# Roped queries and key of latent attention: another row order in DRAM scratch, and weight requests moved into the rope stage

## The chip, the cores and the metric

The kernel runs on one core of a Trainium2 chip. Its time is the device time of one execution in microseconds (us); lower is better. Engines are named as in the profile: PE is the tensor engine (PEld its weight loads), DVE the vector engine, ACT the scalar engine, POOL the GpSimd engine, SP the sync engine. SP computes nothing here and issues transfers; ACT and POOL issue some too, between their own instructions. The engines run side by side, each takes its own instructions in a fixed order, and an instruction that waits holds up all that stand behind it on its engine.

## The reference

Two transformer blocks in float32, one sequence of 512 tokens, width 1024. The change touches only the first layer's mixer, multi-head latent attention with 16 heads:

```python
def mla_mixer(x, positions, cos, sin, w_in, q_norm, kv_norm, w_uq, w_uk, w_uv, w_o):
    h = x @ w_in
    c_q, c_kv, k_r = jnp.split(h, [MLA_Q_LORA, MLA_Q_LORA + MLA_KV_LORA], axis=-1)
    c_q = rms_norm(c_q, q_norm)
    c_kv = rms_norm(c_kv, kv_norm)
    q = (c_q @ w_uq).reshape(B, S, MLA_HEADS, MLA_NOPE + MLA_ROPE)
    q_nope = q[..., :MLA_NOPE]
    q_rope = apply_rope(q[..., MLA_NOPE:], cos[:, :, None], sin[:, :, None])
    k_rope = apply_rope(k_r, cos, sin)
    k_nope = (c_kv @ w_uk).reshape(B, S, MLA_HEADS, MLA_NOPE)
    v = (c_kv @ w_uv).reshape(B, S, MLA_HEADS, MLA_V)
    ...
        s = (jnp.einsum('bqhd,bkhd->bhqk', q_nope[:, q0:q1], k_nope[:, :q1])
             + jnp.einsum('bqhr,bkr->bhqk', q_rope[:, q0:q1], k_rope[:, :q1])).astype(jnp.float32) * scale
    ...
    return (o @ w_o).astype(x.dtype)
```

Each head's score is a sum over 128 plain dimensions and 64 roped ones. The roped key is one for all heads. Behind this mixer follow layer norms, a convolutional feed-forward layer, a second layer with gated linear attention, and a second block with attention, a recurrence and 16 experts; the change leaves all of that alone.

## The kernel before

Every float32 operand of a product is split into a leading part (hi) and an exact rest (lo). A product is three passes on PE, hi\*hi + hi\*lo + lo\*hi (`mm3`, lines 287 to 293). Weights come from DRAM into one of three raw buffers of 128 x 2048 (`load`, line 280, queue SP), and ACT (line 94) and DVE (line 95) split them piece by piece into one of five pairs `wh`, `wl`. A raw buffer is given back when its last piece is split, a pair when its last product is done. `next(w)` forces the split of what a product needs; `prime(n)` asks for the next n tiles early, if a buffer and a pair are free.

Attention (`mla`) runs in this order. The first product (`w_mla_in`) gives the query latents (4 tiles), the key and value latents (2 tiles) and the roped part of the key, each normed and split. The key's part is roped on 64 partitions (lines 537 to 539), copied to the other 64 (line 540) and split, so that `ks`, hi and lo, holds it twice over the partitions. Then the rope stage, `mla_rope`, runs for four groups of four heads. Its two products of 12 matmuls give x1 and x2 of four heads, 32 dimensions each, so that a tile's partition is head\*32 + dimension. DVE rotates them (lines 605 to 610), ACT and DVE split them (lines 270 and 271), and four transfers on SP (line 613) write hi x1, hi x2, lo x1, lo x2 to the scratch `q_dram`, where a head owns 128 rows: 32 of each part, one part behind the other. The head stage follows, 16 times: `mla_qk` reads the head's 128 rows from `q_dram` (line 622, SP) and makes query and key from `w_qk`; `mla_scores` multiplies (lines 666 to 670; the last two use the rows from `q_dram` and `ks`), takes the row maximum (line 676), the exponential (line 679) and the quotient (line 681) for four query tiles of 128, 256, 384 and 512 keys; `mla_transpose` turns the result (line 694) and splits it; `mla_values` multiplies with the values. The next head's query and key are made between a head's scores and its transposes.

`w_qk` is loaded two heads at a time (768 KB), `w_uv` four heads at a time, both through the same raw buffers as the rope weights. On each queue the order of the instructions is set when the program is built, by a scheduler that goes by when it expects buffers and engines to be free; what is asked for earlier in the code tends to be issued earlier. A transfer's wait can also be for an earlier transfer with which it shares a completion semaphore: there are eight of these for the transfers of SP and ACT together, taken in turn. The eight transfers of the input `xT` at the start of the head stage (line 550) are issued on ACT's queue.

Names in the rows below: `ps` a PSUM bank, `r` and `b` slots of 128 x 512 for split operands or float data, `f` quarters of float buffers, `wh`, `wl` weight parts, `raw` raw weights.

Of the kernel before, what the change touches and what calls it, by code (L numbers as in the profile page):

```python
# [55 lines left out]
# columns of the per-channel parameters, 128 channels to a column  # L56
# [10 lines left out]
class Weights:  # L67
    """Weights [group][128, units] taken tile by tile, `kt` units to a tile; split into parts in pieces of some units,
    a piece given back when its last tile is done."""
# [32 lines left out]
    # split what the next n tiles need, as far as there is room  # L102
# [11 lines left out]
class WeightTile:  # L114
# [9 lines left out]
    # all of its units, of a tile in one piece  # L124
# [6 lines left out]
    # of its units up to k  # L131
# [8 lines left out]
class Feed:  # L140
    """Tiles of several weights in a given order, the next ones being split while one is used."""
# [14 lines left out]
class Kern:  # L156
# [66 lines left out]
    # pairs of neighbouring slots: held, they aren't given out one by one; taken, they are out of the pool  # L223
# [40 lines left out]
    # hi keeps the leading mantissa bits that one float32r pass carries, lo is the exact rest  # L264
# [21 lines left out]
    # passes hi*hi + hi*lo + lo*hi  # L286
# [8 lines left out]
    # one output tile (of the depth tiles ks), for the tokens t0..t1  # L295
# [9 lines left out]
    # feature-major product, weights stationary. The first `lead` tiles leave the last depth tiles, which  # L305
    # come late, for the end; the first `head` and last `tail` tiles go by token halves.
    # then: the weights that come next
# [37 lines left out]
    # (v + eps)^-1/2: exp(-ln/2) with one Newton step  # L345
# [8 lines left out]
    # one function table for logarithms and exponentials  # L354
# [3 lines left out]
    # v^-1/2 of a small tile: the exponent halved in integers, then Newton steps  # L358
# [12 lines left out]
    # sum over the partitions of the squares of the tiles, times the value held in `ones`;  # L371
    # the tensor engine takes the squares by groups, of which VectorE makes the sums
# [18 lines left out]
    # layer norm of r without its bias, in r; h, l: the split of the whole  # L391
# [27 lines left out]
    # rms norm of x (kept); h, l the split of the result  # L419
# [15 lines left out]
    # ------------------------------------------------------------------  # L435
    def setup(self):
# [16 lines left out]
        # alpha * ln1 bias  # L453
# [3 lines left out]
    # cos and sin of positions * inv_freq, feature-major; also the block mask  # L457
    def rope_tables(self):
# [19 lines left out]
        # chunk ids; bias[q, k] = -1e30 where the key's chunk lies beyond the query's  # L478
# [13 lines left out]
    def mla(self, q_dram, after):  # L492
# [41 lines left out]
        # roped key, twice over the partitions, hi and lo  # L534
# [5 lines left out]
        nc.scalar.activation(kr[64:], k1, AF.Copy)  # L540
        ks = self.split_new(kr)
        self.free(kr, kt)
# [41 lines left out]
    # output projection of four heads, added to the residual; a tile at a time  # L584
# [13 lines left out]
    # roped parts of four heads' queries, scaled and split, to DRAM as [hi x1; hi x2; lo x1; lo x2] of each head  # L598
    def mla_rope(self, g, st):
        nc, w = self.nc, st["wr"]  # L600
        dst = st["q_dram"].rearrange("(g h i p) n -> g i h p n", g=4, h=4, i=4)
        cos, sin = st["cs"]
        pa = [self.mtile(next(w), 4, st["cq"]) for _ in range(2)]
        ra, rb, t1, t2 = self.Fs(4)
# [29 lines left out]
    # values of two heads, token-major, two token tiles to a slot  # L634
# [13 lines left out]
    # softmax of the scores; key tiles up to the query's  # L648
# [65 lines left out]
    def ffn(self, layer, ups, r, xh, xl, after):  # L714
# [4 lines left out]
        # m: 2 * i for the value, 2 * i + 1 for the gate  # L719
# [38 lines left out]
        for part, kt in enumerate(FF_PARTS):  # L758
# [4 lines left out]
            # one value and gate ahead of the product that waits for the last hidden tile  # L763
# [14 lines left out]
    # x + sigmoid(x @ w_gate + b) * (p @ w_proj); r, without the bias b2, is overwritten  # L778
# [38 lines left out]
    def gla(self, w, xh, xl, r_dram, after):  # L817
# [10 lines left out]
        # decays: log-sigmoids cumulated within each chunk  # L828
# [26 lines left out]
        def ev(m, ps, t0, t1):  # L855
            p, j = divmod(m, 4)
            h = 2 * p + j % 2
            if j < 2:
                q[h] = self.F()
                nc.scalar.activation(q[h], ps, AF.Copy, scale=float(128 ** -0.5))  # L860
            else:
                # decayed keys, token-major
                nc.vector.tensor_tensor(kd[h], kd[h], ps, ALU.mult)
                ps = self.ps("at")
                for t in range(4):
                    nc.tensor.transpose(ps[:, t * P:t * P + P], kd[h][:, t * P:t * P + P], self.ident)
                kdt[h] = self.F()
                nc.vector.tensor_copy(kdt[h], ps)
                self.free(kd[h])
# [4 lines left out]
        def turned(p, t, oc):  # L874
            # [chunk, half of the values, head, token]
# [9 lines left out]
        # states of two heads over the chunks; outputs normed, feature-major  # L885
        def recurrence(p, v):
# [18 lines left out]
            for n in range(8):  # L905
# [4 lines left out]
                # a head to each half of the partitions, a chunk to each half of the columns  # L910
# [63 lines left out]
        # the decays' first product, 16 columns wide: next to their hi parts the lo parts, which so need no pass  # L974
# [34 lines left out]
    def first_block(self, q_dram, r_dram, done):  # L1009
# [3 lines left out]
        for layer in range(2):  # L1013
# [13 lines left out]
            if layer == 0:  # L1027
                r = self.mla(q_dram, ln1)
            else:
                r = self.gla(w_gla, *x, r_dram, ln1)  # L1030
# [22 lines left out]
    # ------------------------------------------------------------------  # L1053
    # token-major copy of x, to DRAM
# [12 lines left out]
    # lambda on every partition  # L1067
# [18 lines left out]
    # rope tables with the norm gains in them: A = [g1 c | g2 c], B = [g1 s | -g2 s] for q and k  # L1086
# [32 lines left out]
    # token-major product of 256 columns, two token tiles to a bank  # L1119
# [11 lines left out]
    # queries and keys of a head: roped with their gains; keys are normed, queries are left to the scores' scale  # L1131
    def qk_head(self, w, then, h, tabs, st):
# [9 lines left out]
        for tp in range(2):  # L1142
            # [token, (tile of the pair, q or k, sub-head, dim)]
# [12 lines left out]
            # hi and lo parts; the transposes stack queries as [hi; hi] and [lo; lo], keys as [hi; lo]  # L1156
# [89 lines left out]
    # rms norm of each head's output over its value dimension  # L1246
# [16 lines left out]
    # softplus(-lambda) * 8, with log1p as an odd series in e / (2 + e)  # L1263
    def lru_consts(self):
# [19 lines left out]
        # half of 8 * softplus, and its negative; half biases  # L1284
# [7 lines left out]
    # gated recurrences of one tile of 128 channels; sigmoids as (1 + tanh) / 2  # L1292
    def lru_tile(self, m, px, pg, raw, y_dram):
        nc, a = self.nc, self.a
        sp, nsp, ba, bi = self.lru_c
        # 2 * gelu(g) = g * (1 + tanh(sqrt(2/pi) (g + 0.044715 g^3)))
# [17 lines left out]
        for d in range(2):  # L1314
# [9 lines left out]
            # z = 8 softplus r; a = exp(-z), 1 - a^2 = tanh(z) (1 + a^2)  # L1324
# [22 lines left out]
    # the recurrent branch, and of the gates as many tiles as FILL_GATES  # L1347
# [21 lines left out]
    # 2 * sigmoid - 1 of one tile of the gates  # L1369
# [12 lines left out]
    def second_block(self, x, h, o_dram, y_dram, g_dram):  # L1382
# [45 lines left out]
        # 2 * sigmoid as 1 + tanh; the halves are taken when merged is split  # L1428
# [32 lines left out]
    # the first block and its norm, x to DRAM token-major, then the second block up to the merged branches  # L1461
    def blocks(self, q_dram, r_dram, xtok, o_dram, y_dram, g_dram):
# [7 lines left out]
        x = self.first_block(q_dram, r_dram, done)  # L1470
        return self.second_block(x, h, o_dram, y_dram, g_dram)

    # ------------------------------------------------------------------
    # x + merged @ w_out, token-major, then its rms norm and the routing
    def out_and_route(self, mh, ml, w, xtok, out):
# [22 lines left out]
        # sum with x, its squares, its part of the router's products without the norm  # L1498
# [62 lines left out]
    def route_setup(self):  # L1561
# [12 lines left out]
        # the last slot less the token id, and its negative  # L1574
# [11 lines left out]
    # one-hot of the first position that holds the maximum  # L1586
# [9 lines left out]
    # group and experts of the tokens of a tile, their places in the experts' queues  # L1596
    def route(self, t, lg, rs):
# [14 lines left out]
        # the two experts of every group, the group of every token  # L1612
# [7 lines left out]
        # an expert's tokens from the first slot on, the others from the last one down  # L1620
# [9 lines left out]
    # weights of the two experts: softmax over them, times the group's probability  # L1630
    def route_weights(self):
# [19 lines left out]
        # token id, one, weight hi, weight lo  # L1651
# [5 lines left out]
    # tokens of the fullest expert  # L1657
# [9 lines left out]
    # [token, slot] of four experts, 1 where the token sits in the slot  # L1667
# [14 lines left out]
    # tokens of the slots, feature-major, split; token ids and weights of the slots  # L1682
    def dispatch(self, g, oh):
        nc = self.nc
        x = []
        for k in range(8):
            # of the first group, some tiles already have the tokens that are routed first
# [17 lines left out]
    # product of an expert's tokens with one of its two first matrices  # L1705
# [36 lines left out]
    # the first products of an expert run before the last of the expert before  # L1742
# [33 lines left out]
    # experts with more tokens than the slots of the first pass: the further slots, 128 at a time  # L1776
# [207 lines left out]
```

## Time and profile before

| what | value |
|---|---|
| median of 3 runs | 2432.88 us (2431.99 to 2433.94) |
| span of the profiled execution | 2430.5 us |
| PE busy | 2359.0 us (97%) |
| DVE busy, ACT busy, POOL busy | 1675.9, 1300.3, 50.1 us |
| mean granted clock of PE | 0.989 of full speed |
| HBM read, written | 286.00 MB, 25.17 MB |

For the profiled execution the page gives the span from its first to its last instruction and no other time; the span is 2.4 us below the median of the runs. PE is busy nearly throughout: in the page's 40 slices of 61 us it has nines everywhere but in the first two and the last, and the second slice, with 5, is the lowest. A busy share of PE near 1 says that the order of the work behind it passes on any shift in time unchanged.

### The profile page before, as it was taken

To read this page: it belongs to the slowest core of one execution; us is meant where nothing else is said; L and a number is where in the kernel's file an instruction comes from. 1 tells how busy PE (TensorE), PEld (TensorE's weight loads), DVE (VectorE), ACT (ScalarE), POOL (GpSimd) and SP (SyncE) were. 2 spreads that over 40 slices of the span, in tenths; PEclk is the share of its full clock that TensorE was granted. 3 is DMA by queue.
4 is the path that set the end of the run, shared out by engine and by line. 5 is a ranking of instruction groups with operands and counts; after the bars stand their busy time and mean duration, and the time that the engine had idled before them with its cause. 6 is when DMAs were issued, how large, how long until landed. Compare 5 with 4: busy or idle time off the path is not lost. (4 is left out here: it accounts for less than half of the span.)

```text
span 2430.5 us, 31858 instructions
## 1 busy us (share of the span) xinstructions
PE 2359.0 (97%) x12252; PEld 1987.2 (82%) x12252; DVE 1675.9 (69%) x3236; ACT 1300.3 (54%) x2048; POOL 50.1 (2%) x52
## 2 busy tenths in 40 slices
PE   8599999999999999999999999999999999999997
PEld 6488888888889776798888899888888778788886
DVE  7476668646466645585554578888888664989876
ACT  5154444434245523353332466777777843678776
POOL 0000000000000000000000000000000000011001
PEclk9799999999999999999999999999999999999999
DMA  5421221232222322312222213222323254489887
GB/s 182 146 76 66 78 100 41 99 109 100 104 96 88 118 78 83 117 70 98 104 93 104 98 69 123 101 91 76 118 70 109 74 199 165 176 310 380 300 302 246
DMA packets 62475, 313.26 MB, mean 129 GB/s; under 512 B 7504, under 2 KB 8144, under 8 KB 33904
## 3 DMA queue, kind: packets, MB, share of 16 engines
q1 hardware_dynamic: 49200, 279.73, 31.6%
q0 software_dynamic: 4864, 16.78, 2.7%
q10 hardware_dynamic: 8256, 14.68, 2.0%
q8 instruction: 98, 1.61, 0.3%
q14 instruction: 57, 0.47, 0.1%
HBM read 286.00 MB, written 25.17 MB: 128 GB/s over the span
## 5 line engine op out<-in xcount | busy, mean ns | idle before, releaser
L291 PE MATMUL ps<-r,wh 128*128 128x512 f32 (+1 forms) x2352 | 865.2, 371 | 14.0 <-ACT r L268 7.6
L293 PE MATMUL ps<-r,wl 128*128 128x512 f32 (+1 forms) x2352 | 862.3, 368 | 2.7 <-DVE wl L95 2.6
L292 PE MATMUL ps<-r,wh 128*128 128x512 f32 (+1 forms) x2320 | 851.9, 368 | 1.1 <-DVE r L269 0.5
L94 ACT ACTIVATE wh<-raw 128x1024 fp32r<-128x1024 f32 (+2 forms) x416 | 426.9, 1033 | 564.5 <-PE ps L292 433.4
L95 DVE TENSOR_TENSOR wl<-raw,wh 128x1024 fp32r<-128x1024 f32 (+2 forms) x416 | 491.6, 1191 | 213.5 <-ACT wh L94 206.5
L291 PEld LDWEIGHTS ps<-r,wh 128*128 128x128 f32 x2352 | 444.1, 190 | 92.6 <-ACT r L268 8.0
L293 PEld LDWEIGHTS ps<-r,wl 128*128 128x128 f32 x2352 | 444.5, 189 | 75.8 <-DVE wl L95 4.2
L292 PEld LDWEIGHTS ps<-r,wh 128*128 128x128 f32 x2320 | 438.9, 190 | 75.2 <-issue 3.9
L291 PE MATMUL ps<-wh,r 128*128 128x512 f32 (+1 forms) x944 | 325.6, 345 | 0.0
L292 PE MATMUL ps<-wl,r 128*128 128x512 f32 (+1 forms) x944 | 323.1, 342 | 1.9 <-DVE wl L95 1.9
L293 PE MATMUL ps<-wh,r 128*128 128x512 f32 (+1 forms) x944 | 323.6, 343 | 0.0
L292 PEld LDWEIGHTS ps<-wl,r 128*128 128x128 f32 x944 | 179.3, 190 | 23.0 <-DVE wl L95 2.6
L291 PEld LDWEIGHTS ps<-wh,r 128*128 128x128 f32 x944 | 179.2, 190 | 21.1 <-issue 1.2
L293 PEld LDWEIGHTS ps<-wh,r 128*128 128x128 f32 x944 | 179.2, 190 | 20.6 <-issue 0.8
L95 DVE TENSOR_TENSOR wl<-f,wh 128x1024 fp32r<-128x1024 f32 x96 | 113.7, 1222 | 10.2 <-ACT wh L94 8.9
L94 ACT ACTIVATE wh<-f 128x1024 fp32r<-128x1024 f32 x96 | 98.8, 1059 | 19.9 <-PE ps L293 19.9
L268 ACT ACTIVATE r<-ps 128x512 fp32r<-128x512 f32 (+1 forms) x141 | 76.0, 572 | 59.5 <-PE ps L293 42.1
L269 DVE TENSOR_TENSOR r<-ps,r 128x512 fp32r<-128x512 f32 (+1 forms) x132 | 83.4, 657 | 32.6 <-ACT r L268 32.4
L268 ACT ACTIVATE r<-f 128x512 fp32r<-128x512 f32 (+1 forms) x105 | 60.9, 589 | 59.5 <-DVE f L744 23.5
L269 DVE TENSOR_TENSOR r<-f,r 128x512 fp32r<-128x512 f32 (+1 forms) x105 | 65.7, 637 | 30.6 <-ACT r L268 28.1
L743 ACT ACTIVATE f<-f 128x512 f32<-128x512 f32 x39 | 24.7, 633 | 73.0 <-DVE f L727 72.9
L724 ACT ACTIVATE f<-ps,par 128x512 f32<-128x512 f32 (+1 forms) x78 | 56.8, 731 | 9.3 <-PE ps L293 9.3
(530 smaller groups left out, 2795.2 us busy)
## 6 DMA issues: line engine op xcount, KB each, us to landing
raw<-w_ffn_up SPq DMA_DIRECT2D x44, 1024.0 KB
f<-w_exp_in SPq DMA_DIRECT2D x33, 1024.0 KB
raw<-w_exp_in SPq DMA_DIRECT2D x31, 1024.0 KB
raw<-w_exp_dn SPq DMA_DIRECT2D x17, 1024.0 KB
raw<-w_ffn_dn SPq DMA_DIRECT2D x16, 1024.0 KB
f<-w_exp_dn SPq DMA_DIRECT2D x15, 1024.0 KB
raw<-w_gla SPq DMA_DIRECT2D x17, 512.0 KB
raw<-w_mla_o SPq DMA_DIRECT2D x8, 1024.0 KB
```

Source lines behind the costliest of these rows:

```text
L94: k.nc.scalar.activation(h, src, AF.Copy)
L95: k.nc.vector.tensor_tensor(l, src, h.bitcast(F32), ALU.subtract)
L268: nc.scalar.activation(h, src, AF.Copy)
L269: return nc.vector.tensor_tensor(l, src, h.bitcast(F32), ALU.subtract).ins
L291: self.nc.tensor.matmul(out, ah, bh, start=f, stop=False)
L292: self.nc.tensor.matmul(out, ah, bl, start=False, stop=False)
L293: self.nc.tensor.matmul(out, al, bh, start=False, stop=e)
L724: nc.scalar.activation(t[:, t0:t1], ps, AF.Identity, bias=self.col("conv_b", layer * m2 + ch), scale=w(2))
L743: nc.scalar.activation(g, g, AF.Gelu_apprx_tanh)
```

## The change

It has three parts.

1. The order of rows in the scratch: a head's 128 rows are now ordered by dimension first and part last (dimension\*4 + part). Each of the four writes of a group then covers 128 rows at a step of four, one run from partition 0 to 127, where it was four blocks of 32 rows.
2. The roped key has to have its rows in the same order. It is split on 64 partitions into `kp`, written from POOL's queue to a new scratch `k_dram` in eight transfers of 32 rows (each part once for the query's hi and once for its lo), and read back in two transfers of 128 rows into `ks`. The copy to the other 64 partitions is gone.
3. Within `mla_rope`, the third and fourth group ask for the first and the first two tiles of `w_qk` once their products are issued.

Lines that only held comments are emptied, so the code behind shifts by up to nine lines.

```diff
-        nc.scalar.activation(kr[64:], k1, AF.Copy)
-        ks = self.split_new(kr)
-        self.free(kr, kt)
+        kp, ks = self.Rs(2), self.Rs(2)
+        self.split(k1, kp[0][:64], kp[1][:64])
+        kd = k_dram.rearrange("(z p j i) n -> z j i p n", z=2, j=2, i=2)
+        for z in range(2):
+            for j in range(2):
+                for i in range(2):
+                    nc.gpsimd.dma_start(kd[z, j, i], kp[z][i * 32:i * 32 + 32].bitcast(F32))
+            nc.gpsimd.dma_start(ks[z].bitcast(F32), k_dram[z * P:z * P + P, :])
+        self.free(kr, kt, kp)
...
     def mla_rope(self, g, st):
         nc, w = self.nc, st["wr"]
-        dst = st["q_dram"].rearrange("(g h i p) n -> g i h p n", g=4, h=4, i=4)
+        dst = st["q_dram"].rearrange("(g p i) n -> g i p n", g=4, i=4)
         cos, sin = st["cs"]
         pa = [self.mtile(next(w), 4, st["cq"]) for _ in range(2)]
+        if g > 1:
+            st["wqk"].prime(g - 1)
```

How the rows move on SP, from the end of the rope stage of the kernel before (L613 are the writes of roped queries, L622 the read of one head's rows, L280 a load of weights):

```order
L622 DMA r_85<-q_dram 128x512
L613 DMA q_dram<-r_87 4x32x512
L613 DMA q_dram<-r_91 4x32x512
L613 DMA q_dram<-r_89 4x32x512
L613 DMA q_dram<-r_93 4x32x512
L280 DMA raw_69<-w_qk 128x1536
L280 DMA raw_67<-w_uv 128x1024
L280 DMA raw_68<-w_mla_o 128x2048
```

The same place now (the write is L622, the read L631):

```order
L622 DMA q_dram<-r_87 128x512
L280 DMA raw_69<-w_qk 128x1536
L622 DMA q_dram<-r_85 128x512
L622 DMA q_dram<-r_89 128x512
L280 DMA raw_68<-w_qk 128x1536
L631 DMA r_89<-q_dram 128x512
L622 DMA q_dram<-r_91 128x512
L280 DMA raw_67<-w_uv 128x1024
L622 DMA q_dram<-r_95 128x512
```

The load of `w_qk` for heads 4 and 5 stood behind all 16 writes (`raw_69`) and stands now behind 12 of them (`raw_68`); the one for heads 2 and 3, which was issued ahead of the rope stage, is now `raw_69`, behind ten.

On ACT, where the rope stage begins, before (L268 splits the key, L270 the roped queries, L94 weights; L550 are transfers of `xT`):

```order
L94 ACTIVATE wh_74<-raw_67 128x512
L540 ACTIVATE b_123<-b_123 64x512
L550 DMA f_80<-xT 128x512
L268 ACTIVATE r_113<-b_123 128x512
L270 ACTIVATE r_115<-f_82 128x512
```

and now (the transfers of `xT` are L556):

```order
L94 ACTIVATE wh_74<-raw_68 128x768
L268 ACTIVATE r_113<-b_123 64x512
L556 DMA f_80<-xT 128x512
L556 DMA b_123<-xT 128x512
L94 ACTIVATE wh_76<-raw_67 128x512
L270 ACTIVATE r_117<-f_82 128x512
```

The split of the first values' weights, `wh_76`, now stands ahead of the first split of roped queries; its pair is in use until the second group's products are done. Further on, at the first head's softmax, ACT before (L268 splits key and values, L679 is the exponential):

```order
L268 ACTIVATE r_94<-ps_129 128x512
L679 ACTIVATE f_84,s_680<-f_84,s_679 128x128
L679 ACTIVATE f_84,s_680<-f_84,s_679 128x384
L679 ACTIVATE b_122,s_680<-b_122,s_679 128x256
L94 ACTIVATE wh_74<-raw_69 128x768
L679 ACTIVATE f_84,s_680<-f_84,s_679 128x512
```

and now (the exponential is L688):

```order
L268 ACTIVATE r_98<-ps_129 128x512
L94 ACTIVATE wh_76<-raw_68 128x768
L688 ACTIVATE f_84,s_692<-f_84,s_691 128x128
L688 ACTIVATE f_84,s_692<-f_84,s_691 128x384
L688 ACTIVATE b_122,s_692<-b_122,s_691 128x256
L688 ACTIVATE f_84,s_692<-f_84,s_691 128x512
```

The split of the weights of head 4 (`wh_74<-raw_69` before, `wh_76<-raw_68` now) moved from ahead of the fourth exponential to ahead of the first. From the middle of the head stage to the end of the program the order on all engines is the same, but for buffer numbers.

## Rows read from the trace of the kernel before

**Rows 1.** Waits of the computing engines, 50 to 140 us: total us, times, longest.

```profile
PE ps L694 <- DVE f L681: 30.0, 1, 30.0
...
ACT wh L94 <- DMA raw<-w_qk: 30.0, 1, 30.0
...
ACT wh L94 <- DMA q_dram<-r: 8.1, 1, 8.1
...
DVE b L271 <- ACT b L270: 4.9, 1, 4.9
...
PE ps L291 <- DVE b L608: 2.4, 1, 2.4
```

**Rows 2.** Timeline of ACT, 60 to 123 us: start, duration, instruction, idle time before it.

```profile
60.59 0.64 ACT L268 ACTIVATE r<-b 128x512 fp32r<-128x512 f32 x1
62.33 0.64 ACT L270 ACTIVATE r<-f 128x512 fp32r<-128x512 f32 x1 [1.10 <-DVE f L609]
...
122.21 0.84 ACT L94 ACTIVATE wh<-raw 128x768 fp32r<-128x768 f32 x1 [30.01 <-DMA raw<-w_qk]
122.96 0.71 ACT L679 ACTIVATE f<-f,s 128x512 f32<-128x512 f32 x1
```

**Rows 3.** Timeline of SP's queue, 62 to 110 us.

```profile
62.99 4.70 SPq L613 DMA_DIRECT2D q_dram<-r  x4
...
105.99 3.06 SPq L613 DMA_DIRECT2D q_dram<-r  x4
109.15 2.74 SPq L280 DMA_DIRECT2D raw<-w_qk  x1
```

**Rows 4.** Windows: length; busy us (instructions) of PE, PEld, DVE, ACT, POOL; clock; DMA share; GB/s.

```profile
95.26:125.26 30.00, 0.00 (x0) 0.00 (x1) 1.47 (x4) 3.03 (x6) 0.00 (x0) 0.56 0.43 155
125.26:129.40 4.14, 4.14 (x13) 3.46 (x14) 3.36 (x6) 1.36 (x3) 0.00 (x0) 0.50 0.01 2
129.40:133.50 4.10, 4.10 (x29) 3.96 (x28) 1.69 (x7) 0.66 (x2) 0.00 (x0) 1.00 0.00 0
80.90:85.00 4.10, 3.66 (x12) 2.75 (x13) 4.07 (x7) 2.29 (x4) 0.00 (x0) 0.59 0.45 105
140.00:200.00 60.00, 60.00 (x336) 52.53 (x335) 43.41 (x122) 30.14 (x66) 0.00 (x0) 1.00 0.25 83
72.00:74.00 2.00, 2.00 (x10) 1.69 (x9) 2.00 (x4) 0.00 (x0) 0.00 (x0) 1.00 0.26 101
806.00:808.00 2.00, 2.00 (x11) 1.65 (x10) 2.00 (x4) 0.47 (x2) 0.00 (x0) 1.00 1.00 350
```

**Rows 5.** Timeline of SP's queue, 804 to 807 us: a weight load and a write of 128x512.

```profile
804.14 0.33 SPq L280 DMA_DIRECT2D raw<-w_gla  x1
806.68 0.32 SPq L1045 DMA_DIRECT2D r_dram<-f  x1
```

**Rows 6.** Timeline of PE, 90 to 126 us: scores, next head's query and key, transposes.

```profile
90.22 0.40 PE L670 MATMUL ps<-r,r 128*128 128x512 f32 x1
90.45 0.39 PE L291 MATMUL ps<-r,wh 128*128 128x512 f32 x1
...
94.54 0.27 PE L694 MATMUL ps<-ident,f 128*128 128x128 f32 x1
...
94.97 0.27 PE L694 MATMUL ps<-ident,f 128*128 128x128 f32 x1
125.26 1.33 PE L694 MATMUL ps<-ident,f 128*128 128x128 f32 x5 [30.02 <-DVE f L681]
```

**Rows 7.** Timeline of DVE: the maximum of the first head's fourth tile.

```profile
91.47 0.68 DVE L676 CUSTOM_DVE_ANT_0 f<-ps,f 128x512 f32<-128x512 f32 x1
```

**Rows 8.** Timeline of POOL: its first transfer, and a later one.

```profile
1476.30 0.75 POOL L1064 DMA_DIRECT2D xtok<-f  x1 [1475.84 <-ACT f L1063]
...
1536.56 0.54 POOL L1364 DMA_DIRECT2D g_dram<-f  x1 [38.38 <-ACT f L1375]
```

**Rows 9.** Landing of POOL's eight writes of 256 KB to one scratch.

```profile
DMA to landing us min/median/max: 2.3/2.3/5.5
```

More of the change, by code (lines that the diff above doesn't have):

```diff
@@ L489, in rope_tables, with mla @@
         return cos, sin, bias, fs
-    def mla(self, q_dram, after):
+    def mla(self, q_dram, k_dram, after):
         nc, a = self.nc, self.a
@@ L1007, in gla, with first_block @@
         return r
-    def first_block(self, q_dram, r_dram, done):
+    def first_block(self, q_dram, k_dram, r_dram, done):
         a = self.a
@@ L1027, in first_block @@
             if layer == 0:
-                r = self.mla(q_dram, ln1)
+                r = self.mla(q_dram, k_dram, ln1)
             else:
@@ L1459, in second_block, with blocks @@
         return mh, ml, w_out
-    def blocks(self, q_dram, r_dram, xtok, o_dram, y_dram, g_dram):
+    def blocks(self, q_dram, k_dram, r_dram, xtok, o_dram, y_dram, g_dram):
         h = []
@@ L1469, in done @@
             self.store_tokens(r, xtok, t0, t1)
-        x = self.first_block(q_dram, r_dram, done)
+        x = self.first_block(q_dram, k_dram, r_dram, done)
         return self.second_block(x, h, o_dram, y_dram, g_dram)
@@ L1850, in body @@
         new = lambda n, rows, cols: dram.tile([rows, cols], F32, tag=n, name=n)
-        q_dram, xtok = new("q_dram", 16 * P, S), new("xtok", S, D)
+        q_dram, k_dram, xtok = new("q_dram", 16 * P, S), new("k_dram", 2 * P, S), new("xtok", S, D)
         r_dram, o_dram, y_dram = (new(n, D, S) for n in ("r_dram", "o_dram", "y_dram"))
         g_dram = new("g_dram", 2 * D, S)
-        m = k.blocks(q_dram, r_dram, xtok, o_dram, y_dram, g_dram)
+        m = k.blocks(q_dram, k_dram, r_dram, xtok, o_dram, y_dram, g_dram)
         k.rings(mm=4, lg=1, at=3)
```

## The prediction

> **What bounds the kernel now.** I read the slices of the page first: PE is at nine tenths or more nearly everywhere, with one hole in the second slice. Then windows around it: PE runs no instruction in 30.00 us, and then 4.14 us at a granted clock of 0.50 (the level of 1.2 GHz) before it is back at 1.00 (2.4 GHz) [rows 4]. Further on, from 140 us, PE is full in every microsecond of the head stage [rows 4]. So the hole's length is the question.
>
> The list of waits then says who holds whom [rows 1]. PE's transposes wait 30.0 us for DVE's quotient (L681). That waits for the fourth exponential, and this one stands on ACT behind a weight split that waits 30.0 us for a load of `w_qk`. The timelines date it: the split starts at 122.21 and the exponential right behind it [rows 2], the last five transposes at 125.26 [rows 6]. The load was issued on SP at 109.15, behind the last four writes of roped queries (from 105.99) [rows 3]. So the bound is SP's queue.
>
> Why the writes are slow stands in the windows: with nothing but writes of the form 4x32x512 under way (72 to 74 us) the transfer engines are 0.26 busy and move 101 GB/s; at 806 to 808 us, with a weight load and a write of 128x512 issued shortly before [rows 5], they are 1.00 busy and move 350 GB/s [rows 4]. There are sixteen writes of 128 x 512 values of four bytes, four to a group. At 101 GB/s one takes 262144 / 101000 = 2.6 us, all sixteen 41.5 us. They begin at 62.99, and 62.99 + 41.5 = 104.5 is about where the last group is issued [rows 3].
>
> **The change part by part.** *The writes.* Each covers 128 rows now. By the row of 806 us, 256 KB at 350 GB/s take 0.75 us, sixteen 12 us. The step of four rows in DRAM is in no row; the bounds are 101 and 350 GB/s, and I take 350, since in the old form too the runs in DRAM are 2 KB rows, and what differs between the two windows is the share of the engines (a quarter, or all). Here the Trainium skill bears ("DMA: Bandwidth & Descriptors", section "Why a DMA increments its semaphore by 16 and not by 1"): a transfer is spread over the largest number of engines, up to 16, that divides the slowest dimension of both sides. By that rule the old form gets 4 of 16 and the new one 16; the share of 0.26 agrees for the old one, and by it the sixteen would take about a quarter of 41.5 us, 10 us.
>
> *The load that ends the wait.* On SP it stands behind 12 writes, not 16. What it must wait for is the split of the piece that was in its buffer, and the writes ahead of it, each of which waits for its own split on ACT and DVE. In the old trace ACT and DVE were themselves held back by slow writes: ACT waited 8.1 us for one at a shared semaphore, DVE 4.9 us for ACT, and PE 2.4 us for DVE [rows 1]. PE had worked without a gap up to 80.9 - 2.4 = 78.5 [rows 1, 4], at 0.227 us a matmul (18 of them from 90.45 to 94.54 [rows 6]); so the products of the third group, with 36 matmuls behind them (24 of the fourth, 12 of the first query), end at 70.3. Some ten instructions of DVE at 0.68 us [rows 7] split that group and the weights in its buffer, by about 77.5. The load is then out before 80, and 768 KB at 350 GB/s take 2.2 us. It lands before 86, and ACT needs it at about 87, ahead of the first exponential (the scores' last matmul is followed by the next product at 90.45 [rows 6]). So this wait goes.
>
> *What is late next.* For the last five transposes it is either PE's own work or the softmax of the fourth tile. In the old run PE had finished everything ahead of them at 94.97 + 0.27 = about 95.3 [rows 6], with the wait of 2.4 us in it. The softmax: DVE's maximum of the fourth tile ends at 91.47 + 0.68 = 92.15 [rows 7], and from the exponential's start to the transposes it took 125.26 - 122.96 = 2.3 us [rows 2, 6]; with one weight split of 0.84 us [rows 2] in between, 95.3. Both say 95.3, so 125.26 - 95.3 = **30.0 us** go. Without the wait of 2.4 us PE would be there at 92.9.
>
> *The clock.* After the hole PE ran 4.14 us at 0.50. Without a hole this is done in half: **2.1 us** go. Before it, too, PE was slow: 0.59 from 80.90 to 85.00, behind the wait of 2.4 us [rows 4]; at full clock that costs 4.10 x 0.41 = 1.7 us less. I leave it in, for the following reason.
>
> *The order on ACT and PE.* The split `wh_76` now stands ahead of the first split of roped queries, which ran at 62.33 [rows 2]. Its pair is free when the second group's products end. That is 24 matmuls of 0.227 us before 70.3, at 64.9, so the split of the first group's queries moves to about 65.7, 3.3 us later. DVE takes its work in order and is nearly full here, so its reading of the banks of the third group comes 2 to 3 us later, and PE, whose next product needs them, waits some 3 to 4 us in pieces of about 1 us. The wait of 2.4 us that goes is nearly as long, so I set the two against each other at zero: bounds a gain of 2.4 + 1.7 = 4.1 us (no wait, no slow clock), a loss of 6 us (waits of 8.4 us in place of 2.4, the clock down as long as before).
>
> *The key.* ACT's copy of the key to the other partitions is gone: one instruction beside other work, nothing. Ten transfers on POOL, which is idle here (its first transfer comes at 1476.30 [rows 8]): an issue takes 0.54 us, the first 0.75 [rows 8], a landing 2.3 to 5.5 us [rows 9]. The key's split on ACT ran at 60.59 [rows 2], so it begins at about 61.3. Eight writes, with the first read behind the first four and the second behind the rest: 10 x 0.54 + 2 x 5.5 = 16.4 us at most if only landings in a chain count, so `ks` is there by 78. The first score matmul that reads it is the fourth of twenty, which end at 90.45 [rows 6], so it comes near 87.5. Nothing, with 9 us to spare. The read of head 1's rows on SP waits for four of these writes (it takes their buffer); it stands behind the second group's writes at about 73, when they have landed.
>
> Sum: 30.0 + 2.1 + 0 = 32.1 us. The span goes from 2430.5 to 2398.4; the runs' median lies 2.4 above the span, so **2400.8 us**. Nothing gives it back: from 140 us on PE is full and the order is the old one, so the rest shifts as a whole.
>
> **Rivals.** *A, the writes stay at 101 GB/s* (the step of four rows decides, and the change doesn't do what it says). For it: no row shows that step. Against it: a quarter of the engines is what the old form shows. The load would still stand before four of the writes: 4 x 2.6 = 10.4 us earlier, 2422.
>
> *B, the hole is filled by a new wait.* ACT has its weight splits ahead of exponentials and query splits, each waiting for a load or a pair; one that comes 8 to 14 us late keeps that much of the hole, 2409 to 2415. For it: such a wait made the old hole. Against: three loads of 768, 512 and 768 KB and the writes need some 20 us at 350 GB/s between 62 and 90 us.
>
> *C, slower: the key's way through DRAM on POOL.* If each of its ten transfers waits for the one before, 10 x (0.54 + 5.5) = 60.4 us, `ks` lands at 121.7, and the scores start 34 us late. PE would stand idle through that, and the clock would fall as after the old hole (2.1 us): 2400.8 + 34 + 2 = 2437. It decides from a chain of 26 us on (61.3 to 87.5), and costs more than the rest gains from 58 us on. For it: nothing on POOL moved this early in the old run. Against: the order issues four writes in a row, and 256 KB landed in 2.3 us in the median. The Trainium skill has a rule for it ("SBUF — State Buffer", section "SBUF: two separate sides"): GpSimd can't write descriptors while DVE runs certain copies at its faster rate. No run here shows this.
>
> *D, no wait at all*: the gain of 4.1 us comes on top, 2396.7. For it: DVE loses no time to ACT any more. Against: the split of values' weights ahead of the queries'.
>
> **How the numbers follow.** Forecast with its own range of 2397 to 2408: 0.74. D or a little more, 2393 to 2397: 0.08 (further waits that I don't see could go with it). B 0.08, A 0.04, C and other losses 0.04, the rest within 0.2% of before (about 5 us, what runs of this kernel can tell from no change) 0.02. The range of 2395 to 2410 takes in the bounds of the small waits and leaves out rivals A, C and most of B. Faster by over 0.2%: 0.94; within: 0.02; slower: 0.04.
>
> **What would show it.** Right: writes at about 300 GB/s and a DMA share near 1 between 65 and 80 us; no wait of ACT for `w_qk` over 2 us; the last transposes of head 0 at 94 to 98 us; the clock at 1.00 from 100 us on. Wrong: a wait of PE at the first scores for `ks` (C), ACT at a weight split for over 5 us (B), or writes at a share of 0.26 (A).

## The result and the profile after

The changed kernel takes 2404.78 us (median of 4 runs, 2398.74 to 2406.5), the kernel before 2432.43 us beside it; the ratio is 0.9881 (95% interval 0.9867 to 0.9895). Predicted were 2400.8 us, in a range of 2395 to 2410. Taken once more on another chip it was 2403.45 us, ratio 0.9874 (0.9859 to 0.9889). The profiled execution has a span of 2404.3 us, 26.2 less than before.

First the windows, with the columns of [rows 4]: the hole of 30.00 us is gone. In its place stands a short hole of PE at 82.80, with a slow clock behind it.

```profile
65.00:70.00 5.00, 5.00 (x23) 4.14 (x23) 5.00 (x9) 1.24 (x2) 0.91 (x2) 1.00 1.00 338
72.00:74.00 2.00, 2.00 (x11) 1.64 (x10) 2.00 (x3) 1.17 (x2) 0.57 (x1) 1.00 1.05 404
75.00:80.00 5.00, 5.00 (x24) 4.02 (x22) 4.48 (x8) 0.63 (x1) 0.00 (x0) 1.00 1.00 354
82.80:86.22 3.42, 0.28 (x3) 0.07 (x1) 1.20 (x2) 3.23 (x6) 0.00 (x0) 1.00 0.62 227
86.22:94.50 8.28, 7.62 (x25) 6.50 (x26) 5.89 (x20) 3.53 (x9) 0.00 (x0) 0.59 0.62 194
94.50:98.03 3.53, 3.53 (x19) 2.93 (x18) 3.53 (x10) 2.62 (x7) 0.00 (x0) 1.00 0.39 111
1468.00:1476.00 8.00, 6.20 (x22) 4.96 (x22) 7.65 (x28) 4.52 (x11) 0.54 (x1) 0.79 0.50 175
2064.00:2068.00 4.00, 4.00 (x12) 3.17 (x11) 3.98 (x12) 2.79 (x7) 0.00 (x0) 0.58 0.01 4
```

From 72 to 74 us, where the old writes moved 101 GB/s at a share of 0.26, the share is 1.05 and the rate 404 GB/s. The waits of 55 to 130 us, as in [rows 1], say who holds whom now:

```profile
ACT wh L94 <- DMA raw<-w_qk: 6.1, 1, 6.1
...
PE ps L675 <- ACT r L268: 3.1, 1, 3.1
...
PE ps L676 <- DVE r L269: 0.7, 1, 0.7
...
PE ps L291 <- DVE f L616: 0.4, 1, 0.4
```

PE waits 4.2 us in all from 64 to 130 us (32.8 before), at a mean granted clock of 0.95. The first scores (L675) wait for head 0's query and key, which ACT copies from PSUM (L268); ACT waits for a load of `w_qk`. The timelines of SP, ACT and PE, as in [rows 3], [rows 2] and [rows 6], date the three:

```profile
62.91 5.23 SPq L622 DMA_DIRECT2D q_dram<-r  x5
68.31 3.11 SPq L622 DMA_DIRECT2D q_dram<-b  x3
73.15 0.81 SPq L631 DMA_DIRECT2D r<-q_dram  x2
...
75.17 0.33 SPq L280 DMA_DIRECT2D raw<-w_qk  x1
75.60 1.68 SPq L622 DMA_DIRECT2D q_dram<-r  x2
77.38 0.63 SPq L280 DMA_DIRECT2D raw<-w_qk  x1
```

```profile
61.63 0.63 ACT L94 ACTIVATE wh<-raw 128x512 fp32r<-128x512 f32 x1 [2.13 <-DVE f L617]
62.25 0.63 ACT L270 ACTIVATE r<-f 128x512 fp32r<-128x512 f32 x1
...
76.22 0.63 ACT L94 ACTIVATE wh<-raw 128x512 fp32r<-128x512 f32 x1 [3.05 <-PE ps L292]
82.97 0.84 ACT L94 ACTIVATE wh<-raw 128x768 fp32r<-128x768 f32 x1 [6.11 <-DMA raw<-w_qk]
83.83 0.60 ACT L270 ACTIVATE r<-ps 128x512 fp32r<-128x512 f32 x1
...
87.53 0.86 ACT L94 ACTIVATE wh<-raw 128x768 fp32r<-128x768 f32 x1
```

```profile
86.22 0.72 PE L675 MATMUL ps<-r,r 128*128 128x128 f32 x3 [3.15 <-ACT r L268]
...
98.03 0.71 PE L703 MATMUL ps<-ident,f 128*128 128x128 f32 x5
```

The load issued at 77.38 is the one that made the old hole (heads 4 and 5). Its split at 87.53 does not wait. The load issued at 75.17 is that for heads 2 and 3. ACT's order has the split of head 2 right ahead of head 0's query and key, though its product comes two heads later. ACT was free for it at 76.86 and had to wait until 82.97. So the last five transposes start at 98.03, not at 95.3 as forecast (125.26 before).

### The profile page after: what moved, and what is told of

Read it like the earlier page. It is cut to its first block, busy times and chain, and to the rows that moved or that the text cites. A ratio compares the mean times of both kernels' runs of the same rounds, so it can differ in the third digit from the quotient of the medians.

```text
span 2404.3 us, 31885 instructions
## 1 busy us (share of the span) xinstructions
PE 2360.8 (98%) x12252; PEld 1989.0 (83%) x12252; DVE 1676.1 (70%) x3236; ACT 1300.1 (54%) x2047; POOL 55.2 (2%) x62
## 5 line engine op out<-in xcount | busy, mean ns | idle before, releaser
L94 ACT ACTIVATE wh<-raw 128x1024 fp32r<-128x1024 f32 (+2 forms) x416 | 427.0, 1033 | 538.2 <-PE ps L292 445.2
L94 ACT ACTIVATE wh<-f 128x1024 fp32r<-128x1024 f32 x96 | 98.8, 1059 | 19.9 <-PE ps L293 19.8
L268 ACT ACTIVATE r<-ps 128x512 fp32r<-128x512 f32 (+1 forms) x139 | 75.4, 574 | 60.9 <-PE ps L293 44.0
L268 ACT ACTIVATE r<-f 128x512 fp32r<-128x512 f32 (+1 forms) x105 | 60.8, 588 | 57.7 <-DVE f L753 23.5
```

Of the source, the lines that this page charges most:

```text
L94: k.nc.scalar.activation(h, src, AF.Copy)
L268: nc.scalar.activation(h, src, AF.Copy)
```

## The experiments

Theory R: the rows carry the gain, because a write in the new form uses all transfer engines. Theory P: the early request carries it. For the rest that was not gained, theory T1: the load lands late because too much is transferred at once; theory O: it is late because of its place on SP behind the writes. Each time stands beside runs of the kernel before on the same chip (2431.98 to 2433.87 us).

### Each part alone

e1, the kernel before with the early request alone:

```diff
         pa = [self.mtile(next(w), 4, st["cq"]) for _ in range(2)]
+        if g > 1:
+            st["wqk"].prime(g - 1)
```

> The kernel before with only the early request of w_qk (two lines in mla_rope); the writes of roped queries and the key's way are the old ones. Theory R (the rows carry the gain: a write that uses all transfer engines is what empties the queue): the load for heads 2 and 3 now stands behind ten slow writes, 63 + 10 x 2.6 = 89 us, lands after 91, and ACT's split of it stands ahead of head 0's evacuations, which are due at 82.8; the writes still hold back ACT and DVE. So a hole of 8 us or more stays beside the old small waits: 2414 to 2430. Theory P (the early request carries it, the rows hardly matter): 2402 to 2408, as the changed kernel.

e2, the changed kernel without these two lines:

> The changed kernel without the early request. The load for heads 2 and 3 is then issued ahead of all writes, the one for heads 4 and 5 behind all sixteen. Theory R with the landing time (the 3.8 us wait of PE and the slow clock behind it come from a load that the early request put among the writes): no wait at 82.8 us; the load for heads 4 and 5 is issued at 78 to 80 and lands by 88, its split is due at about 92: 2397 to 2401, that is 4 to 7 us below the changed kernel. Theory P (the early request is what takes the old wait away): ACT waits again ahead of the fourth exponential, 2410 to 2432. No difference (2404.8) would say that the wait has another cause.

Measured: e1 2424.34 us, ratio 0.9967 (0.9956 to 0.9979); e2 2402.80 us, 0.9879 (0.9864 to 0.9895). The rows alone bring what both bring together, the early request alone about 8 us, and on top of the rows nothing that can be measured. Theory P falls. ACT in e1, then ACT and the queue of SP in e2:

```profile
103.22 0.84 ACT L94 ACTIVATE wh<-raw 128x768 fp32r<-128x768 f32 x1 [26.73 <-DMA raw<-w_qk]
```

```profile
92.43 0.84 ACT L94 ACTIVATE wh<-raw 128x768 fp32r<-128x768 f32 x1 [5.85 <-DMA raw<-w_qk]
93.18 0.70 ACT L686 ACTIVATE f<-f,s 128x512 f32<-128x512 f32 x1
```

```profile
82.68 0.32 SPq L629 DMA_DIRECT2D r<-q_dram  x1
83.12 3.19 SPq L620 DMA_DIRECT2D q_dram<-r  x4
86.41 0.41 SPq L280 DMA_DIRECT2D raw<-w_qk  x1
```

In e1 the old hole has only moved to another split: its load went out at 90.35, as expected, but the split started at 103.22. In e2 the wait stands at its old place ahead of the fourth exponential, 5.85 us long. My expectation of 2397 to 2401 for e2 was missed. I had the load issued at 78 to 80, but it went out at 86.41, behind a read of roped queries (82.68) and the last four writes (from 83.12), and landed 6.0 us later. So the request inside the rope stage trades one late load for another.

### Why the old writes were slow

e4 leaves the old places in DRAM and cuts each write by heads; e7 takes 2 MB of other traffic (eight loads of `xT`) away from the old writes, by the edit shown for e3 below:

```diff
-            nc.sync.dma_start(dst[g, i], t.bitcast(F32))
+            for h in range(4):
+                nc.sync.dma_start(dst[g, i, h], t[h * 32:h * 32 + 32].bitcast(F32))
```

> The kernel before with each write of 4x32x512 cut into four of 32x512, one for each head: 64 writes, the same places in DRAM, the old key. Theory E (a write is spread over as many engines as divide its slowest dimension: 4 of 16 in the old form, 16 for 32 rows): the share in 70 to 75 us is above 0.7 and the writes end by 85; 2398 to 2406. Theory L (the old writes were slow because a head's part is only 32 rows and the next lies 128 rows further): the share stays near 0.26, 2430 to 2434. Between (2408 to 2420) if SP's issue of 64 transfers takes the place of the slow writes.

> The kernel before (old rows, old key, no early request) with only the loads of xT behind head 1's first copies. Theory R (the old writes are bound by their own form, a quarter of the engines): the share from 65 to 90 us stays near 0.26 and the hole stays, 2429 to 2434. If the old writes were slow because xT's 2 MB shared the engines with them: 2420 or less.

Measured: e4 2404.57 us, 0.9888 (0.9873 to 0.9903); e7 2429.46 us, 0.9985 (0.9975 to 0.9994). A window of e7, then one of e4 and its queue on SP:

```profile
70.00:75.00 5.00, 5.00 (x24) 4.14 (x23) 4.77 (x9) 1.73 (x3) 0.00 (x0) 1.00 0.26 103
```

```profile
65.00:70.00 5.00, 5.00 (x24) 4.14 (x23) 4.72 (x9) 2.82 (x4) 0.00 (x0) 1.00 0.92 294
...
85.00:90.00 5.00, 5.00 (x24) 4.14 (x23) 2.19 (x3) 1.20 (x2) 0.00 (x0) 1.00 0.50 119
```

```profile
62.34 15.51 SPq L614 DMA_DIRECT2D q_dram<-r  x28
77.97 8.25 SPq L614 DMA_DIRECT2D q_dram<-b  x16
86.32 9.31 SPq L614 DMA_DIRECT2D q_dram<-r  x20
```

Without `xT` beside them the old writes stay at a share of 0.26 and 103 GB/s: it is their form. The amount has a small part in it: e7 is faster than the kernel before by more than its interval (0.9985), and its load for heads 4 and 5 goes out at 105.69, 3.5 us earlier. The same rows in pieces of 32 run at twice the old share (0.50, second window of e4). What seems to limit them then is SP, which issues them one behind the other, 20 in 9.31 us (the last row), 0.47 us for 64 KB. So they end at 95.6, where theory E had 85, and the share from 70 to 75 us is 0.70, where it had more than 0.7; the time is in its range. So it is neither the run of 32 rows nor the step in DRAM. How many engines took part is not in the trace, which has only the share of all sixteen. The Trainium skill's rule ("DMA: Bandwidth & Descriptors", section "Why a DMA increments its semaphore by 16 and not by 1": as many engines as divide the slowest dimension) agrees with the shares of e7 (0.26) and the changed kernel (1.00), and with that of e4 in so far as 0.50 is more than a quarter.

### Place or amount

e3 asks for `xT` later, behind head 1's first copies on ACT:

```diff
-        for m in range(8):
-            nc.scalar.dma_start(r[m], a["xT"][m * P:(m + 1) * P, :])
...
                 qk = self.mla_qk(i + 1, st)
+            if i == 0:
+                with self.tc.issue_after(self.last_copy):
+                    for m in range(8):
+                        nc.scalar.dma_start(r[m], a["xT"][m * P:(m + 1) * P, :])
```

> The changed kernel with its eight loads of xT (2 MB) requested on ACT's queue behind head 1's first key and value copies, some 30 us later. Theory T1 (w_qk landed late, 7.8 us after its issue, because 60 to 85 us hold more transfers than they can carry: share 1.00 from 65 to 80 us): with 2 MB less there, w_qk for heads 2 and 3 lands before 80 us, ACT's wait of 6.11 us and PE's of 3.8 us go, and the slow clock behind them: 2397 to 2400. Theory T3 (it is the order of the splits on ACT, or the key's way over POOL, not the amount): 2403 to 2407, PE's wait at 82.8 us stays.

Measured: 2395.52 us (2395.36 to 2396.31), 0.9851 (0.9836 to 0.9866), better than both kernels and 1.5 us under the range of T1. From 64 to 130 us PE waits 0.5 us and its clock is 1.00. But the edit did more than take traffic away: the scheduler now has the load for heads 2 and 3 ahead of all writes, at 55.80. SP, then ACT:

```profile
55.80 0.33 SPq L280 DMA_DIRECT2D raw<-w_qk  x1
63.13 0.92 SPq L624 DMA_DIRECT2D q_dram<-r  x2
...
77.01 0.59 SPq L280 DMA_DIRECT2D raw<-w_qk  x1
```

```profile
85.31 0.84 ACT L94 ACTIVATE wh<-raw 128x768 fp32r<-128x768 f32 x1
```

So three runs try to part the two. e6 is e3 with that load held behind the twelfth write (the SP requests of `mla_qk(2)` queued behind the tenth); in the changed kernel it stands behind ten, not twelve. e5 is e3 without the early request. e9 is the changed kernel, `xT` early, with that load ahead of the writes:

```diff
# e6
-                qk = self.mla_qk(i + 1, st)
+                with self.tc.issue_after(self.tenth_write) if i == 1 else nullcontext():
+                    qk = self.mla_qk(i + 1, st)
# e9, in mla_rope behind the early request
+        if g == 3:
+            w_qk = st["wqk"]
+            w_qk.early = self.load(w_qk.w[1])
```

> e3 with the load of w_qk for heads 2 and 3 held behind the twelfth write again, as in the changed kernel; xT stays late. It is issued at 77 to 78. Theory T1 (the amount): without xT it lands in 3 us, before 81.5, and ACT's split, due at 80, waits 1.5 us at most: 2395 to 2399. Theory O (the place behind the writes): it takes 5 to 8 us to land, ACT waits 4 us or more ahead of head 0's key, 2400 to 2404; the load for heads 4 and 5, now behind all writes, may add 2 us in both.

> The changed kernel without the early request and with the loads of xT behind head 1's first copies. SP's order is that of e2 (heads 4 and 5 behind all sixteen writes, issued there at 86.41, landed at 92.4). Theory T1 (the amount of transfers from 60 to 85 us): the reads and writes in front of that load end earlier, it is issued by 84 and lands by 88, ACT waits under 2 us for it: 2395 to 2398, as e3. Theory O (the place on SP behind the writes decides, whatever else is under way): ACT waits 4 to 6 us again, 2400 to 2403, as e2.

> The changed kernel with the load of w_qk for heads 2 and 3 ahead of all writes; xT early, as there. There are three buffers for raw weights, so w_uv takes the later place on SP, behind ten writes, and its split on ACT stands ahead of head 0's evacuations as the other did. If the wait belongs to the place and the traffic and not to w_qk: ACT waits 3 to 6 us for w_uv, 2401 to 2405. If it was w_qk's load alone: no wait at 80 us, 2396 to 2399.

Measured: e6 2401.88 us, 0.9868 (0.9852 to 0.9885); e5 2398.05 us, 0.9856 (0.9839 to 0.9872); e9 2401.13 us, 0.9867 (0.9851 to 0.9884). ACT in e6, in e5 and in e9:

```profile
84.13 1.58 ACT L94 ACTIVATE wh<-raw 128x768 fp32r<-128x768 f32 x2 [2.57 <-DMA raw<-w_qk]
...
92.10 0.84 ACT L94 ACTIVATE wh<-raw 128x768 fp32r<-128x768 f32 x1 [5.24 <-DMA raw<-w_qk]
```

```profile
88.39 0.85 ACT L94 ACTIVATE wh<-raw 128x768 fp32r<-128x768 f32 x1 [2.51 <-DMA raw<-w_qk]
```

```profile
81.91 1.15 ACT L95 ACTIVATE wh<-raw 128x512 fp32r<-128x512 f32 x2 [8.55 <-DMA raw<-w_uv]
```

The table has, for loads that stand behind writes in the new form, the issue on SP, the time when ACT was free for the split (its start less its wait), and the landing (issue plus the trace's time to landing; with * the start of the waiting split):

| kernel | load | issued | ACT free | landed | issue to landing | ACT waits |
|---|---|---|---|---|---|---|
| changed | w_qk 2, 3 | 75.17 | 76.86 | 82.97 | 7.8 | 6.1 |
| changed | w_qk 4, 5 | 77.38 | 87.53 | 86.1 | 8.7 | 0 |
| changed, again | w_qk 2, 3 | 75.78 | 77.08 | 84.2 | 8.4 | 7.1 |
| e11, reads on POOL | w_qk 2, 3 | 73.78 | 76.94 | 81.86* | 8.1 | 4.9 |
| e8, key on ACT | w_qk 2, 3 | 77.94 | 78.49 | 84.8 | 6.9 | 6.4 |
| e9 | w_uv | 75.67 | 73.36 | 81.9 | 6.2 | 8.6 |
| e6, xT late | w_qk 2, 3 | 78.03 | 81.56 | 84.1 | 6.1 | 2.6 |
| e6, xT late | w_qk 4, 5 | 85.03 | 86.86 | 92.0 | 7.0 | 5.2 |
| e2 | w_qk 4, 5 | 86.41 | 86.58 | 92.4 | 6.0 | 5.9 |
| e5, xT late | w_qk 4, 5 | 81.66 | 85.88 | 88.4 | 6.7 | 2.5 |
| e3, xT late | w_qk 4, 5 | 77.01 | 85.3 | 82.8 | 5.8 | 0 |

A load that stands behind writes lands 5.8 to 8.7 us after its issue, with or without `xT`; for heads 2 and 3 it is 7.8 and 8.4 us with `xT`, behind ten writes, and 6.1 without, behind twelve, so the amount may make about 2 us of it. What differs more is the time from the issue to the place of its split on ACT: 1.7 us in the changed kernel, 8.3 in e3. In e3 and e6 that place is another one. ACT copies head 0's query and the first half of its key ahead of the split for heads 2 and 3, in the changed kernel behind it. ACT in e6, ahead of the wait of 2.57 us:

```profile
79.34 0.60 ACT L270 ACTIVATE r<-ps 128x512 fp32r<-128x512 f32 x1 [3.93 <-PE ps L293]
...
80.96 0.60 ACT L268 ACTIVATE r<-ps 128x512 fp32r<-128x512 f32 x1
```

So PE waits only 0.2 us at the first scores of e6, where the changed kernel lost 3.8. What e6 loses is the other load, for heads 4 and 5, which now stands behind all sixteen writes: PE waits 3.9 us for the softmax behind its split. Its time is in theory O's range, but e6 doesn't hold all the rest fixed.

The amount alone is seen best between e2 and e5, which have nearly the same order on SP. The load for heads 4 and 5 goes out 4.75 us earlier in e5, since the reads and writes ahead of it end earlier, and though it takes no less to land (6.7 us against 6.0) ACT's wait falls from 5.9 to 2.5 us and PE's waits from 5.9 to 2.4. The ratio falls from 0.9879 to 0.9856, 5.6 us. The time is 0.05 us above the range of T1, the wait above its 2 us. From e5 to e3, where the request in the rope stage comes on top, the ratio falls by 0.0005 only, less than the intervals can tell. e9 has the place on SP alone, and gains nothing that can be told from the changed kernel: with three buffers one load must stand behind the writes, and whichever it is, the split that comes too soon on ACT waits, here 8.55 us (3 to 6 were expected).

So T1 is right that less traffic helps, and wrong in how: the load lands little faster once issued, it is issued earlier or its split stands later. How e3's gain divides among the amount, the place on SP and the order on ACT stays open.

### The key, and SP's queue

e8 gives the key its old way; e11 and e10 request the reads of roped queries on POOL's queue, in the changed kernel and in e3 (`nc.gpsimd.dma_start(qr...)` for `nc.sync.dma_start(qr...)`).

```diff
-        kp, ks = self.Rs(2), self.Rs(2)
...
+        nc.scalar.activation(kr[64:], k1, AF.Copy)
+        ks = self.split_new(kr)
```

> The changed kernel with the old way of the key (ACT's copy to the other partitions, no transfers on POOL). The key's rows then stand in another order than the queries', so the roped part of the scores is a product of unlike rows; the work is the same. Prediction, step key: nothing waits for the key, so only its 1 MB of traffic at 59 to 75 us goes. Theory T1 (the amount of transfers): w_qk lands 2 to 3 us earlier, 2398 to 2402. If the amount does not matter: 2403 to 2406.

> The changed kernel with the reads of roped queries on POOL's queue. On SP they waited 6.7 us, and the load of w_qk for heads 2 and 3 stands behind the first two. Theory T1 (the amount of transfers decides when it lands): the load is issued 2 us earlier among transfers that still fill the engines, lands 1 us earlier at most, 2402 to 2406. Theory Q (SP's queue held by reads makes the load late): it is issued before 72 and lands by 78, no wait at 82.8 us, 2396 to 2400.

> e3 with the reads of roped queries requested on POOL's queue, not on SP's, where they held the writes and loads behind them for 8.1 us (two waits for head 0's and 1's writes to land). e3 has no wait of PE over 0.3 us left before 100 us, so nothing should be late that this brings earlier: 2394 to 2397. Under 2393.5 would say that SP's queue still bound something in e3.

Measured: e8 2402.75 us, 0.9876 (0.9861 to 0.9891); e11 2402.26 us, 0.9874 (0.9859 to 0.9889); e10 2396.92 us, 0.9849 (0.9835 to 0.9862). None differs by more than the intervals from the kernel it was made from (0.9874, 0.9874, 0.9851). The key's way over POOL costs nothing that can be seen; e8's time lies between the two ranges expected. Earlier issue of the load (73.78 in e11) made it land 1.1 us earlier only, as T1 had it; the issue before 72 that theory Q asks for did not come about, so Q was not tried. Moving the reads off SP gains e3 nothing.

### The changed kernel once more

> The changed kernel unchanged, once more. Its profiled execution had two stretches of lower clock (0.76 and 0.82 at 1468 to 1476 us, 0.58 at 2064 to 2068 us), about 2.6 us together, which neither the kernel before nor six of the other kernels show there. If they belong to that execution: they are gone here and the median lies at 2401 to 2404. If they belong to this kernel's phase: they are seen again, and the median stays at 2404 to 2407.

Measured: 2403.45 us (2401.73 to 2404.38). The clock is 1.00 at 1468 to 1476 and at 2064 to 2068 us. So the two slow stretches of the first profile (its last two windows above) belonged to that execution.

## Why the prediction was right

The time lies in the range, 4.0 us above the forecast. By its own steps:

- **The writes** are right: the share is 1.00 and the rate 338 to 404 GB/s, and it is the form of the write, not the rows' step or their run of 32 (rival A is out; e4, e7). That this form works by using fewer engines is argued from the shares, not shown. They share that rate, though, with `xT`, the key and the reads: from 60 to 85 us 8.1 MB moved (198, 338, 395, 354 and 335 GB/s in five stretches of 5 us), where the loads and writes I counted are 6.3.
- **The load that ended the wait** is right for heads 4 and 5: issued at 77.38 (forecast: before 80), landed at 86.1, needed at 87.5. But it landed in 8.7 us, not 2.2. This is the mis-sized term: 768 KB at 350 GB/s, as if only its bytes counted. Alone it takes 4.2 us (e3, issued at 98.72), behind writes 5.8 to 8.7.
- **What is late next** fell by the same term. I followed the load that made the old hole and not the other one for heads 2 and 3, whose split stands at 76.86 on ACT. It landed at 82.97, and PE waited 3.15 and 0.65 us. The transposes gained 27.2 us, not 30.0. It is rival B in small: a new wait of ACT for a load, 6.1 us late rather than 8 to 14, and ahead of the scores rather than of the exponential. "No wait of ACT for `w_qk` over 2 us" is wrong, and the sign set for B, ACT at a weight split for over 5 us, came.
- **The clock**: the 4.14 us at 0.50 behind the old hole are gone, but there are 8.28 us at 0.59 behind the new one (0.50 from 88 to 94 us, 1.00 from 94.5 on). Over 64 to 130 us the clock is 0.95 against e3's 1.00, which is 3.3 us.
- **The small waits** I set at zero, for a reason that did not come: `wh_76` ran at 61.63, so its pair was free 3.3 us before my time for the end of the second group's products (64.9), and the first query split came at 62.25, where it had been [rows 2]; PE lost 0.36 us there. Other waits came: PE's 3.8 us and 3.3 us of slow clock. Set against the old wait of 2.4 us and its slow clock of 1.7 they are a loss of about 3 us, inside the bound of 6. That the range held them is in part luck: its bounds were made for another wait.
- **The key**: rival C is out. POOL's ten requests went out by 73.1 us and PE waited for none of them; e8 is no faster. The Trainium skill's rule on GpSimd's descriptors ("SBUF — State Buffer", section "SBUF: two separate sides") was not put to the test: seven issues took 3.71 us from 59.82 on, 0.53 each, with DVE busy, but DVE ran only `TENSOR_TENSOR` and `SCALAR_TENSOR_TENSOR` there and no copy.

Of the 5.9 us by which the profiled span (2404.3) misses the forecast one (2398.4), 3.4 are there at the first POOL transfer behind the attention: 1476.30 before [rows 8], 1447.56 now, 28.7 us of the 32.1. The other 2.5 are lost behind it, where the slow stretches lie. In the repeat, without them, the gain is 27.9 us there and 28.1 at the end.

The forecast of rival D, no wait at all, was 2396.7 us. e3 comes to about that, at 2395.52, by another order of requests. The sum of what the changed kernel still loses against it from 64 to 130 us is 4.2 - 0.5 us of waits and 3.3 us of clock, 7.0; that POOL transfer comes 7.9 us earlier in e3 (1439.63 against 1447.56). The runs of the changed kernel spread over 2398.74 to 2406.5 us; the slow stretches seen once explain at most 3.4 us of that (8.00 x 0.21 + 4.00 x 0.42), and what decides in which execution they come was not tried.

## What to carry to other kernels

A load's price is the time from issue to landing in the queue that it joins, not its bytes over the bandwidth: 2.2 us by bytes were 4.2 alone and 5.8 to 8.7 behind writes. When a wait goes, list every load that is issued in the stretch and set its landing against the place of its first use on the engine that works in order; the next late one need not be the one that made the old hole. In e2 and the changed kernel, an earlier request only moved one load ahead of another, for the buffers and the queue stayed the same.

## What the runs showed of the hardware that was not expected

- SP's issue is not a fixed cost. It is 0.33 us where little is under way, 0.32 to 0.93 us for each of the sixteen writes of the changed kernel, and 2.3 to 3.0 us for each load in e1, among slow writes. (The first five of those writes, 5.23 us in one row of the queue, have waits for their splits between them, so 5.23 / 5 is no price of an issue.) It looks as if an issue is held while transfers before it are backed up, but no run shows that: the load at 75.17 took 0.33 us at a share near 1.00. A slow write does hold SP through the reads that wait for it: 22.8 us in three waits in the kernel before, 6.7 us in two now.
- PE paused for 3.15 us and, soon after, for 0.65 us, and from 88 to 94 us its granted clock was 0.50, the level of 1.2 GHz. The clock took about as much as the waits themselves. In e5, where the longest wait of PE was 1.7 us, the clock stayed at 1.00.
